# Holding the state-space scan's small matmuls in the program's order on TensorE

## The chip, the cores and the metric

The kernel runs on one core of a Trainium2 chip. The metric is the device time of one execution in microseconds; runs of the same kernel are summed up by their median.

## The reference, cut to what matters

One layer of a hybrid block: dilated attention and a state-space branch in parallel, on 256 positions of width 2048, float32 throughout. The change touches the scan of the state-space branch, which has 8 groups of 8 heads of 64 channels, with a state of 128:

```python
def step(state, inp):
    xc, dac, bc, cc = inp                       # chunks of 128 positions
    acum_t = jnp.moveaxis(jnp.cumsum(dac, axis=1), 1, -1)
    seg = acum_t[..., :, None] - acum_t[..., None, :]
    decay = jnp.exp(jnp.where(causal, seg, -jnp.inf))
    cb = jnp.einsum('blgn,bsgn->bgls', cc, bc)
    y_diag = jnp.einsum('bgls,bgjls,bsgjp->blgjp', cb, decay, xc)
    y_off = jnp.einsum('blgn,bgjpn,blgj->blgjp', cc, state, jnp.exp(acum))
    ...
    return new_state, y_diag + y_off
...
proj = rms_norm(x, norm_w) @ w_in               # q, k, v, z_a, z_s, xbc, dt, g_a, g_s
...                                             # conv and silu on xbc -> xs, B, C; dt = softplus
y = ssd_chunked_scan(xs * dt, dt * a, B, C) + d_skip * xs
y = rms_norm(y * silu(z_s), ssm_norm_w)
merged = sigmoid(g_a) * (o_a @ w_attn_branch) + sigmoid(g_s) * (y @ w_ssm_branch)
return rms_norm(x + merged @ w_out, final_norm_w)
```

The kernel doesn't carry a state from chunk to chunk: with two chunks it multiplies, for each head, the causal 256 x 256 matrix of C, B and decay with the inputs.

## The kernel before, in words

**Weights.** All weights stream from memory in units of 128 x 1024 floats, in one fixed order. ScalarE makes a rounded high part `h` of each unit (line 265) and VectorE the remainder `l` (line 266), into rings of four buffers each; TensorE multiplies with both parts. A projection of 128 output channels (`gemm_a`) reads two units: 16 pairs of an h matmul of 512 columns (line 318) and an l matmul of 256 columns (line 321) into one bank of PSUM.

**Groups.** For each of the 8 groups the program runs projections for B and C (groups 1 to 7), then by turns `xs` and `zs` for its four tiles of 128 channels. Between them stand a few gate projections (`gs`). Each projection begins with a tick of a counter. Work that must lie between projections is put on a list with the number of ticks to wait (`after`), and runs when the counter is there; with `inside=1` it is issued behind the first h matmul of a projection, ahead of that projection's first l matmul.

**The scan of a group.** Three ticks after a group's last `xs` projection has begun, `turn` transposes the inputs and makes `xdt`. `decays` (four calls, from the second tick on) makes the matrices `gt` on ScalarE and, per two calls, one VectorE multiplication (line 760). Eleven ticks after (some more where gate projections stand between), `scan` issues 16 matmuls, all on line 788, into two banks `yp`. Each takes 64 stationary columns, so that it writes 64 partitions: index `j` says which half, and neighbours in the source write different halves. Each is two records in the trace. Behind the scan, `gather` reads the sums on VectorE (line 800).

**What sets the order.** The source gives the program's order. The context is opened with `schedule_with_timeline_sim=True`: the framework simulates a timeline and issues on each engine, whenever that engine is free in the simulation, the first instruction in the program's order that is ready there. So an instruction whose inputs are ready may be issued ahead of its place in the source, into a pause of its engine in the simulated timeline. On the chip each engine then runs its queue in the order so fixed, with semaphores for the data.

Of the kernel before, what the change touches and what calls it, by code (L numbers as in the profile page):

```python
# [186 lines left out]
def hybrid_block(ctx: ExitStack, tc: tile.TileContext, wall, xt, x, pk_d, cst_d, fw_d, out):  # L187
    nc = tc.nc
    ve, ac, gp, pe = nc.vector, nc.scalar, nc.gpsimd, nc.tensor

    lead = ctx.enter_context(tc.tile_pool(name="lead", bufs=1))
    big = ctx.enter_context(tc.tile_pool(name="big", bufs=1))
# [20 lines left out]
    def bank(tag, bufs, name):  # L213
        return ps.tile([P, 512], F32, name=name, tag=tag, bufs=bufs)
# [77 lines left out]
    def after(ticks, f, inside=0):  # L292

        due.append((now[0] + ticks + inside / 2, f))
# [359 lines left out]
    with tc.tile_pool(name="ssm", bufs=2) as sp:  # L654
# [125 lines left out]
        def scan(g, state):  # L780
            xdt, gt = state["xdt"], state["gt"]
            yps = [bank("m2", 2, f"yp{g}_{v}") for v in range(2)]
            for k in (3, 2, 1, 0):
                v, i = divmod(k, 2)
                for a, b, c, o in ((0, S, 0, 0), (S, 384, 1, P)):
                    for j in range(2):
                        n, rows, col = 2 * i + j, 64 * j, i * S + o
                        pe.matmul(
                            yps[v][rows : rows + 64, col : col + b - a], xdt[:, v, c, n, :], gt[:, 4 * v + n, a:b],
                            start=(c == 0), stop=(c == 1),  # L790
                        )
            for v, yp in enumerate(yps):
                after(Y_AFTER[v], lambda a=(2 * g + v, yp, state["xs"][v], state["zs"][v]): gather(*a))

        def gather(u, yp, xs, zs):
            if True:
                y1 = sp.tile([P, 2, S], F32, name=f"y1_{u}", tag="y1", bufs=1)
                for i in range(2):
                    t = 2 * u + i
                    ve.scalar_tensor_tensor(  # L800
                        y1[:, i], xs[:, i], dsk[:, t : t + 1], yp[:, i * S : (i + 1) * S], ALU.mult, ALU.add
                    )
                ve.tensor_tensor(y1, y1, zs, ALU.mult)
                ac.activation(xs, y1, AF.Square)
                ve.tensor_tensor(ssq, ssq, xs, ALU.add)
                if u in (8, 12):
                    yT.append(half_kts(f"yT1{u}", "yo1a" if u == 8 else "yo1b"))
                for i in range(2):
                    t = 2 * u + i
                    split(y1[:, i], kt_of(yT, t)[:, :S], kt_of(yT, t)[:, S:], scale=nw[:, t : t + 1])  # L810
# [65 lines left out]
        for g in range(GROUPS):  # L876
# [9 lines left out]
            for t in range(max(4 * g, 1), 4 * g + 4):  # L886
                u, i = divmod(t, 2)
                acc = project(("xs", t))
                if i == 0:
                    state["xs"].append(new_pair(u, "xs"))  # L890
                if t % 4 == 3:
                    gate = 4 * len(GS_BEFORE.get(g + 1, ()))
                    after(TURN_LAG + gate * 3 // 4, lambda a=(g, state): turn(*a))

                    y_lag = Y_LAG + gate
                    for k in range(4):
                        after(GT_LAG + k if k < 3 else y_lag - 2, lambda a=(g, k, cb, state): decays(*a))
                    after(y_lag, lambda a=(g, state): scan(*a), 1)
                    for q in (2 * g, 2 * g + 1):
                        if q in SX_Y:  # L900
                            after(
                                y_lag + 2 + Y_AFTER[1] + q % 2 * 3,
                                lambda q=q, g=g: keep_left(
                                    ("y", q), two_kts(yT, q), Y_SPARE[q], at if g < 6 else ring(f"sxt_y{q}")
                                ),
                            )
                conv(collect(acc, f"x{t}"), t, state["xs"][-1][:, i], f"x{t}")
                acc = project(("zs", t))
                if i == 0:
                    state["zs"].append(new_pair(u, "zs"))  # L910
                zh = ev.tile([P, S], F32, name=f"zh{t}", tag="eh", bufs=2)
                evac(acc, zh, f"z{t}", scale=0.5)
                half_silu(zh, state["zs"][-1][:, i], f"z{t}")
# [260 lines left out]
```

## Time and profile before

| | |
|---|---|
| median of 3 runs | 1389.33 us (1388.9 to 1390.08) |
| the profiled execution's own time | 1389.12 us |
| its span, first to last instruction | 1387.3 us |
| granted TensorE clock | 0.998 |
| TensorE busy | 1376.8 us, 99% of the span |
| VectorE busy | 1148.3 us, 83% |
| ScalarE busy | 828.9 us, 60% |
| scan matmuls (line 788) | 256 records, first at 164.4 us, last at 584.5 us |

PE is TensorE, PEld its weight loads, DVE is VectorE, ACT is ScalarE, POOL is GpSimd, SP is SyncE. A row of the timeline has the start and the duration in us, then engine, line, operation, the tile written and those read, the shapes, and how many were merged into the row. Matmuls overlap in a pipeline and their ends are modelled, so a matmul's cost is read from start to start. A row of the waits view has who waited for whom, then the total in us, the number of times and the longest.

### The profile page before, as it was taken

The numbers are of one execution on the slowest core, as the hardware profiler recorded it, in microseconds if no ns is written. First come the engines' busy times: TensorE is split into PE (matmuls) and PEld (weight loads), VectorE is DVE, ScalarE is ACT, GpSimd is POOL, SyncE is SP. The second block draws the span as 40 slices with busy tenths as digits, with TensorE's granted clock in tenths as the row PEclk, the third lists the DMA queues.
The fourth block names the chain that finished last, engine by engine and source line by source line (L and its number), as shares of the span: only waits on it lengthen the run. The fifth ranks groups of instructions, "written<-read, shape, count | busy, mean of one in ns | idle before, by whom it ended". The sixth has DMA issues, their size and how long they took to land.

```text
span 1387.3 us, 20558 instructions
## 1 busy us (share of the span) xinstructions
PE 1376.8 (99%) x7272; PEld 1171.5 (84%) x7272; DVE 1148.3 (83%) x1709; ACT 828.9 (60%) x1289; POOL 130.3 (9%) x201
## 2 busy tenths in 40 slices
PE   9999999999999999999999999999999999999997
PEld 7888888888888888888888888888888888888886
DVE  6898998887798888868878997777777688889897
ACT  7656677675677675765554554544544456556464
POOL 2301110010000000010000001111111000000110
PEclk9999999999999999999999999999999999999999
DMA  9766877868676866567767668888888656776764
GB/s 346 231 189 213 285 241 236 272 200 300 217 251 212 261 197 204 186 228 267 237 224 258 224 195 287 275 274 277 296 287 279 182 171 219 270 250 207 251 241 150
DMA packets 100743, 332.67 MB, mean 240 GB/s; under 512 B 11232, under 2 KB 13472, under 8 KB 100512
## 3 DMA queue, kind: packets, MB, share of 16 engines
q1 hardware_dynamic: 99920, 330.18, 72.0%
q8 instruction: 57, 0.93, 0.3%
q10 hardware_dynamic: 720, 1.18, 0.2%
q14 instruction: 46, 0.38, 0.1%
HBM read 306.87 MB, written 24.44 MB: 239 GB/s over the span
## 4 chain that ended last, share of the span: by engine, by line
PE 98%; DMA 0%; DVE 0%; POOL 0%; SPq 0%; ACT 0%; issue 0%; POOLq 0%; DVEq 0%; ACTq 0%
PE ps_zs L318 8%; PE ps_xs L318 8%; PE ps_zs L321 4%; PE ps_q L318 4%; PE ps_k L318 4%; PE ps_za L318 4%; PE ps_xs L321 4%; PE ps_ssm L463 3%; PE ps_ssm L464 3%; PE ps_ssm L465 3%; PE ps_q L321 2%; PE ps_k L321 2%; PE ps_za L321 2%; PE ps_gs L402 2%; PE ps_gs L403 2%; PE ps_gs L401 2%
## 5 line engine op out<-in xcount | busy, mean ns | idle before, releaser
L265 ACT ACTIVATE h<-w 128x1024 fp32r<-128x1024 f32 (+1 forms) x408 | 425.7, 1049 | 357.2 <-issue 82.8
L266 DVE TENSOR_TENSOR l<-w,h 128x1024 fp32r<-128x1024 f32 (+1 forms) x408 | 491.9, 1211 | 160.9 <-ACT h L265 158.5
L318 PE MATMUL ps_zs<-XT,h 128*128 128x512 f32 x496 | 175.7, 395 | 0.0
L318 PE MATMUL ps_xs<-XT,h 128*128 128x512 f32 x496 | 175.2, 394 | 0.0
L321 PE MATMUL ps_zs<-XT,l 128*128 128x256 f32 x496 | 139.6, 282 | 0.0
L321 PE MATMUL ps_xs<-XT,l 128*128 128x256 f32 x496 | 139.6, 281 | 0.0
L318 PEld LDWEIGHTS ps_xs<-XT,h 128*128 128x128 f32 x496 | 93.0, 188 | 21.3
L318 PEld LDWEIGHTS ps_zs<-XT,h 128*128 128x128 f32 x496 | 93.1, 188 | 20.9
L321 PEld LDWEIGHTS ps_zs<-XT,l 128*128 128x128 f32 x496 | 93.6, 189 | 1.9 <-issue 1.1
L321 PEld LDWEIGHTS ps_xs<-XT,l 128*128 128x128 f32 x496 | 93.6, 189 | 0.8 <-issue 0.6
L318 PE MATMUL ps_q<-XT,h 128*128 128x512 f32 x256 | 92.3, 404 | 0.0
L318 PE MATMUL ps_k<-XT,h 128*128 128x512 f32 x256 | 89.8, 394 | 0.0
L318 PE MATMUL ps_za<-XT,h 128*128 128x512 f32 x256 | 89.5, 394 | 0.0
L321 PE MATMUL ps_q<-XT,l 128*128 128x256 f32 x256 | 71.0, 277 | 0.0
L321 PE MATMUL ps_k<-XT,l 128*128 128x256 f32 x256 | 71.0, 277 | 0.0
L321 PE MATMUL ps_za<-XT,l 128*128 128x256 f32 x256 | 70.9, 277 | 0.0
L318 PEld LDWEIGHTS ps_k<-XT,h 128*128 128x128 f32 x256 | 48.0, 188 | 11.1
L318 PEld LDWEIGHTS ps_za<-XT,h 128*128 128x128 f32 x256 | 48.0, 188 | 11.0
L318 PEld LDWEIGHTS ps_q<-XT,h 128*128 128x128 f32 x256 | 48.0, 188 | 10.9
L751 ACT ACTIVATE gt<-acb,acT 128x128 f32<-128x128 f32 x128 | 43.8, 391 | 19.5 <-DMA acb<-acum_d 16.4
L512 ACT ACTIVATE ha<-wa 128x1024 fp32r<-128x1024 f32 x38 | 40.0, 1054 | 20.8 <-DMA wa<-in_wall 7.4
L513 DVE TENSOR_TENSOR ltu<-wa,htu 128x1024 fp32r<-128x1024 f32 x38 | 46.4, 1222 | 5.8 <-ACT htu L512 5.4
(633 smaller groups left out, 3270.2 us busy)
## 6 DMA issues: line engine op xcount, KB each, us to landing
w<-in_wall SPq DMA_DIRECT2D x404, 512.0 KB, 4.5
wa<-in_wall SPq DMA_DIRECT2D x38, 512.0 KB, 4.4
th_a<-in_wall SPq DMA_DIRECT2D x18, 512.0 KB, 5.5
acb<-acum_d SPq DMA_DIRECT2D x32, 256.0 KB, 3.8
wb<-in_wall SPq DMA_DIRECT2D x30, 256.0 KB, 3.7
sums_at<-in_wall SPq DMA_DIRECT2D x12, 512.0 KB, 4.0
t_ssm<-sums_at SPq DMA_DIRECT2D x12, 512.0 KB, 4.3
wt<-t_ssm SPq DMA_DIRECT2D x12, 512.0 KB, 4.9
```

Source lines behind the costliest of these rows:

```text
L265: ac.activation(h[:, a:b], w[:, a:b], AF.Copy)
L266: ve.tensor_tensor(l[:, a:b], w[:, a:b], h[:, a:b].bitcast(F32), ALU.subtract)
L318: pe.matmul(acc, h[:, kk, :], m, start=(kt == 0), stop=False)
L321: pe.matmul(acc[:, S:], l[:, kk, :], m[:, :S], start=False, stop=(kt == KT - 1))
L401: pe.matmul(accs[i], xh, h[:, kk], start=(kt == 0), stop=False)
L402: pe.matmul(accs[i], xh, l[:, kk], start=False, stop=False)
L463: pe.matmul(acc, xh, h, start=start, stop=False)
L464: pe.matmul(acc, xh, l, start=False, stop=False)
L465: pe.matmul(acc, xl, h, start=False, stop=stop)
L512: ac.activation(h, src, AF.Copy)
L513: ve.tensor_tensor(l, src, h.bitcast(F32), ALU.subtract)
L751: ac.activation(g4[:, n, b], acb[:, j, b // 2 * P : b // 2 * P + P], AF.Relu, scale=-1.0, bias=sc[:, h : h + 1],)
```

## The change

Each matmul of the scan is passed through `tc.keep_in_program_order`. That adds an edge from the matmul to the instruction that the source wrote last before it on the same engine. The edge binds the order of issue alone: the matmul may not be issued ahead of that instruction. It adds no semaphore and doesn't wait for the other's result. The first matmul of a scan is thereby bound behind the first h matmul of the projection in which `scan` is called, and each of the other 15 behind the one before it. The instructions that follow the scan in the source are not bound.

```diff
     ve, ac, gp, pe = nc.vector, nc.scalar, nc.gpsimd, nc.tensor
+    in_order = tc.keep_in_program_order
...
                 for a, b, c, o in ((0, S, 0, 0), (S, 384, 1, P)):
                     for j in range(2):
                         n, rows, col = 2 * i + j, 64 * j, i * S + o
-                        pe.matmul(
-                            yps[v][rows : rows + 64, col : col + b - a], xdt[:, v, c, n, :], gt[:, 4 * v + n, a:b],
-                            start=(c == 0), stop=(c == 1),
+                        in_order(
+                            pe.matmul(
+                                yps[v][rows : rows + 64, col : col + b - a], xdt[:, v, c, n, :], gt[:, 4 * v + n, a:b],
+                                start=(c == 0), stop=(c == 1),
+                            )
                         )
```

## Prediction

> **What bounds the kernel now.** I read the page first, then the waits of TensorE, then the timeline of TensorE alone around each place where the scan's matmuls (source line L788, tile `yp`) stand.
>
> ```profile
> span 1387.3 us, 20558 instructions
> ## 1 busy us (share of the span) xinstructions
> PE 1376.8 (99%) x7272; PEld 1171.5 (84%) x7272; DVE 1148.3 (83%) x1709; ACT 828.9 (60%) x1289; POOL 130.3 (9%) x201
> ```
>
> ```profile
> PE warm L592 <- DVE ssq L589: 1.4, 1, 1.4
> PE ps_first L366 <- ACT h L265: 0.7, 1, 0.7
> ```
>
> The first fence says that TensorE's rows cover 99% of the span. The second is the whole answer of the waits view for TensorE: 1.4 + 0.7 = 2.1 us of waiting, once each, both at the very start (warm-up matmuls and the first weight unit). So from there on the end of the kernel is set by what TensorE has in its queue and how long each piece takes. A microsecond taken out of that queue comes off the span, as long as the engines that feed it stay ahead.
>
> The Trainium skill speaks against reading it this way: "Trainium Kernel Development and Optimization", section "Performance Expectations", calls matmul busy time a bad metric because matmuls are pipelined, and names the share of weight loads among the good ones. By that, 84% stands for TensorE, there would be room on the engine, and the change would move nothing (my second case below). The trace's waits say otherwise, 2.1 us in all, and I go by them.
>
> How the scan stands among the projections, undisturbed (group 0; TensorE's timeline, the columns are start, duration, engine, line, operation, tiles, count):
>
> ```profile
> 163.78 0.39 PE L318 MATMUL ps_xs<-XT,h 128*128 128x512 f32 x1
> 164.01 0.28 PE L321 MATMUL ps_xs<-XT,l 128*128 128x256 f32 x1
> 164.12 0.39 PE L318 MATMUL ps_zs<-XT,h 128*128 128x512 f32 x1
> 164.44 2.82 PE L788 MATMUL yp<-gt,xdt 128*64 128x256 f32 x32
> 167.19 0.39 PE L321 MATMUL ps_zs<-XT,l 128*128 128x256 f32 x1
> 167.42 0.39 PE L318 MATMUL ps_zs<-XT,h 128*128 128x512 f32 x1
> ```
>
> The durations overlap, so I count from start to start. The projection's pitch, from one h matmul to the next with the l matmul between, is 164.12 - 163.78 = 0.34 us. With the scan between them the same step is 167.42 - 164.12 = 3.30 us. So one whole scan block (16 matmuls of the source, two records each, 32) costs 3.30 - 0.34 = 2.96 us of TensorE's time. In three groups the 32 don't stand together.
>
> ```profile
> 201.68 0.40 PE L318 MATMUL ps_zs<-XT,h 128*128 128x512 f32 x1
> 202.00 0.65 PE L788 MATMUL yp<-gt,xdt 128*64 128x256 f32 x2
> 202.58 0.39 PE L321 MATMUL ps_zs<-XT,l 128*128 128x256 f32 x1
> 202.80 0.40 PE L318 MATMUL ps_zs<-XT,h 128*128 128x512 f32 x1
> ```
>
> ```profile
> 225.62 0.40 PE L318 MATMUL ps_zs<-XT,h 128*128 128x512 f32 x1
> 225.94 2.81 PE L788 MATMUL yp<-gt,xdt 128*64 128x256 f32 x30
> 228.69 0.39 PE L321 MATMUL ps_zs<-XT,l 128*128 128x256 f32 x1
> 228.91 0.39 PE L318 MATMUL ps_zs<-XT,h 128*128 128x512 f32 x1
> ```
>
> Group 1: one matmul (x2) runs alone, four projections ahead of the other fifteen (x30). The block of 30 takes as long as one of 32.
>
> ```profile
> 260.64 0.39 PE L318 MATMUL ps_zs<-XT,h 128*128 128x512 f32 x1
> 260.96 0.86 PE L788 MATMUL yp<-gt,xdt 128*64 128x256 f32 x6
> 261.75 0.39 PE L321 MATMUL ps_xs<-XT,l 128*128 128x256 f32 x1
> 261.97 0.40 PE L318 MATMUL ps_xs<-XT,h 128*128 128x512 f32 x1
> ```
>
> ```profile
> 287.04 0.39 PE L318 MATMUL ps_zs<-XT,h 128*128 128x512 f32 x1
> 287.36 2.38 PE L788 MATMUL yp<-gt,xdt 128*64 128x128 f32 x26
> 289.67 0.38 PE L321 MATMUL ps_zs<-XT,l 128*128 128x256 f32 x1
> 289.89 0.40 PE L318 MATMUL ps_zs<-XT,h 128*128 128x512 f32 x1
> ```
>
> Group 2: three matmuls (x6) ahead, thirteen (x26) at the block's place.
>
> ```profile
> 523.96 0.39 PE L318 MATMUL ps_zs<-XT,h 128*128 128x512 f32 x1
> 524.27 0.65 PE L788 MATMUL yp<-gt,xdt 128*64 128x256 f32 x2
> 524.85 0.39 PE L321 MATMUL ps_xs<-XT,l 128*128 128x256 f32 x1
> 525.07 0.40 PE L318 MATMUL ps_xs<-XT,h 128*128 128x512 f32 x1
> ```
>
> ```profile
> 350.00:400.00 50.00, 2.82 (x32) 2.00 (x32) 1.00 0.69 221
> 400.00:450.00 50.00, 2.82 (x32) 2.00 (x32) 1.00 0.73 236
> 450.00:500.00 50.00, 2.82 (x32) 2.00 (x32) 1.00 0.73 225
> 500.00:550.00 50.00, 0.65 (x2) 0.19 (x2) 1.00 0.71 219
> 550.00:600.00 50.00, 5.64 (x62) 4.21 (x62) 1.00 0.59 193
> ```
>
> Group 6: again one matmul ahead. The last fence is the windows view of the scan's line (busy time and count on TensorE, then on its weight loads): groups 3, 4 and 5 are whole, and the blocks of 30 (group 6) and of 32 (group 7) are busy 5.64 us together, 2 x 2.82, so this block of 30 too costs what a whole one costs.
>
> **The change, part by part.** It removes, adds and lengthens no instruction. Each scan matmul gets an edge behind the TensorE instruction that the source wrote just before it. Such an edge orders issue only; it adds no semaphore and no wait. The first matmul of a scan is tied behind the first h matmul of the projection in whose midst the source puts the scan, the other fifteen behind one another. No DMA, and no instruction of another engine, is tied.
>
> What must go is the early start in groups 1, 2 and 6: the five matmuls (x2, x6, x2) can't be issued before their block's place any more. What I expect instead is eight blocks of 32.
>
> The sum, start to start, each less the pitch of 0.34:
> - Group 1: early part 202.80 - 201.68 - 0.34 = 0.78; block 228.91 - 225.62 - 0.34 = 2.95; together 3.73 against 2.96 for a whole block. Saved 0.77.
> - Group 2: early part 261.97 - 260.64 - 0.34 = 0.99; block 289.89 - 287.04 - 0.34 = 2.51; together 3.50. Saved 0.54.
> - Group 6: early part 525.07 - 523.96 - 0.34 = 0.77; block 2.96 as shown. Saved 0.77.
>
> In all 0.77 + 0.54 + 0.77 = 2.08 us.
>
> Why a lone matmul is so dear can be seen in the rows. At the whole block's rate two records are 2.96 x 2/32 = 0.19 us; alone they took 0.78. The shape column says 128*64: a scan matmul fills half of the array's columns, and in the source its neighbour fills the other half. Alone, the other half stands empty, and its partner later runs alone too, which is why a block of 30 is no shorter than one of 32. Besides, entering and leaving the half-width shape costs: from the last h start to the first scan start are 202.00 - 201.68 = 0.32 us, where from h to l in the plain stream are 164.01 - 163.78 = 0.23. And the first l after it is followed by h at 202.80 - 202.58 = 0.22, where it is 164.12 - 164.01 = 0.11 in the plain stream.
>
> The Trainium skill, "TensorEngine Tiling (Array Packing)", section "Key Properties", says that changing the tiling mode drains the TensorE. The rows agree: 0.32 against 0.23 us on entering. The page gives no figure for the drain; counting only the array's own time, the sum would be the busy difference that I give next.
>
> Both sides of the 2.08. From below: the busy times of the early parts, 0.65 + 0.86 + 0.65, less what the block of 26 is shorter than one of 32, 2.82 - 2.38 = 0.44, are 1.72 us; this leaves out the pauses of entering and leaving. From above: if the three matmuls put back in group 2 filled idle column halves, as the one in group 1 would, the block of 26 would not grow by 0.45, and the saving would be 2.53. I take 2.08, since the whole block was measured and holds all of its matmuls.
>
> What it costs elsewhere. The moved matmuls run later than now, by 24 us in group 1 and 26 us in group 2; their inputs were there at the early place, so nothing new is waited for at the later one. Each group's sums are read by VectorE after its last scan matmul, and that one stands where it stood. The wait that could newly appear is indirect. The kernel's order on every engine comes from a simulated timeline, in which the early matmuls filled pauses; without them that timeline shifts by some tenths of a microsecond after 202 us, and near-ties on VectorE, ScalarE and SyncE's queue may fall the other way. Ahead of 202 us the order should be unchanged. I cost this at nothing. The cover is the lead with which the weights' low parts are made:
>
> ```profile
> 245.83 1.22 DVE L266 TENSOR_TENSOR l<-w,h 128x1024 fp32r<-128x1024 f32 x1
> ```
>
> ```profile
> 249.35 0.19 PEld L321 LDWEIGHTS ps_xs<-XT,l 128*128 128x128 f32 x1
> ```
>
> These belong to the same unit of weights (counting units and l tiles in order), and this is the smallest lead that I find between 200 and 600 us: ready at 245.83 + 1.22 = 247.05, first loaded at 249.35, 2.30 us ahead. If some reordering delays an l by less than that, TensorE doesn't feel it; beyond it, every microsecond shows.
>
> The profiled execution took 1389.12 us, its span 1387.3 with 1.8 us around it; the median of the runs shown is 1389.33. So 1389.12 - 2.08 = 1387.0 for such an execution, and 1389.33 - 2.08 = 1387.2 for the median.
>
> **The rivals.**
> - *Nothing saved.* Either TensorE is not the bound and the 2.08 us turn into idle time, or the early pauses of the planner are filled by other matmuls of equal cost. Against it: the two waits above, and that the scan's are the only half-width matmuls in this stretch; full-width ones moved forward cost the same wherever they stand. 1389.3.
> - *Slower: the re-planned order makes VectorE late.* Place: VectorE between 202 and 600 us. Its longest pieces there are the multiplications of the decay matrices, two per group:
>
> ```profile
> L760 DVE TENSOR_TENSOR gt<-gt,cb 128x1536 f32<-128x1536 f32 x12 | 21.0, 1752 | 0.4 <-ACT gt L759 0.4
> ```
>
> If the two of a group (2 x 1.75) and the subtraction of another unit (1.22) came ahead of an l with the smallest lead, it would be 4.72 - 2.30 = 2.42 us late, and TensorE would stand for so long. It decides from 2.30 us of work moved ahead; it outweighs the saving from one group on. In three of the six groups from 2 to 7 it would be 7.26 - 2.08 = 5.2 us slower than now: 1394.5. For it: VectorE is busy 83% of the span. Against it: two such multiplications would have to fall together at the worst unit, after a shift of tenths of a microsecond.
>
> **How the numbers follow.** What a measurement of this kernel can tell from no change is about 0.2%, 2.8 us. The forecast, 1387.2, has 0.79; nothing saved 0.08; slower 0.13. The forecast saves 0.15%, within 0.7 us of the bound; the runs shown lie 1.18 us apart (1388.9 to 1390.08) and the saving may be 2.53, so I put a quarter of the forecast, 0.20, beyond it. Faster 0.20; within 0.2%: 0.59 + 0.08 + 0.01 of the slower case = 0.68; slower 0.12. The range: low is 1389.33 - 2.53 - 1.18 = 1385.6; high takes in nothing saved and the slower case with one group late, 1387.2 + 2.42 + 1.18 = 1390.8.
>
> **What would show it.** Right: the scan's line in eight runs of x32, with no x2, x6, x26 or x30, each step from h to h about 3.30; TensorE's waits still 2.1 us; TensorE's instructions as many as before; no difference ahead of 201 us; and group 2's block, after two early parts that are gone (0.78 and 0.99), starting at 287.36 - 1.77 = 285.6. Wrong: pieces of the scan still apart; new rows in TensorE's waits naming l or h; or a wait that isn't there now between 202 and 600 us. If the block's place itself moves within a projection, or the order after 600 us differs and costs, the forecast fails on the step that I costed at nothing.

## The result and the profile after

The changed kernel takes 1387.86 us in the median (22 runs, 1386.87 to 1389.66), the kernel before 1389.59 us (22 runs, 1388.9 to 1390.43). The ratio is 0.9987 with a 95% interval of 0.9981 to 0.9993. That is 1.73 us less, 0.13%, with an interval of 1.0 to 2.6 us: a real gain, but inside the 0.2% that the prediction counted as no change. The forecast was 1387.2 us, and its range, 1385.6 to 1390.8, held the time. Of the 0.66 us between forecast and median, 0.26 are the kernel before: its median over 22 runs is 1389.59, where the forecast had 1389.33 from three. The profiled execution took 1387.36 us against 1389.12 us before.

First the page of the changed kernel, then the whole answer of its waits view for TensorE, then from the waits of the weight loads the two rows that the text uses, and last the row of before that answers to the first of them. All lines of the source stand one to three lower than before: 788 is 790, 318 is 319, 321 is 322.

```profile
span 1385.5 us, 20557 instructions
## 1 busy us (share of the span) xinstructions
PE 1375.6 (99%) x7272; PEld 1171.3 (85%) x7272; DVE 1148.6 (83%) x1709; ACT 829.9 (60%) x1289; POOL 130.0 (9%) x201
```

```profile
PE warm L593 <- DVE ssq L590: 1.4, 1, 1.4
```

```profile
PEld yp L790 <- issue: 2.1, 8, 0.4
...
PEld ps_attn L465 <- DVE l L267: 0.3, 1, 0.3
```

```profile
PEld yp L788 <- issue: 3.1, 11, 0.4
```

TensorE has as many instructions as before, 7272, and still waits for almost nothing. The loads of `yp` paused for issue 11 times before, for 3.1 us in all; now they do so 8 times, once per block. The row of `ps_attn` is new: it has one weight load of the attention branch waiting for a low part `l`.

The scan's own rows, by the windows view of its line over the stretches that hold groups 1 and 2 and groups 6 and 7. The columns are the window, its length, TensorE's busy time and count, that of the weight loads, the clock, the DMA share and the GB/s. The first fence is before, the second after.

```profile
200.00:300.00 100.00, 6.71 (x64) 4.72 (x64) 1.00 0.76 245
500.00:600.00 100.00, 6.28 (x64) 4.40 (x64) 1.00 0.65 206
```

```profile
200.00:300.00 100.00, 5.64 (x64) 4.01 (x64) 1.00 0.75 251
500.00:600.00 100.00, 5.64 (x64) 4.00 (x64) 1.00 0.62 203
```

The same 128 records are busy 12.99 us before and 11.28 us after, 1.71 us less. Each stretch now costs twice 2.82 us. TensorE's timeline of the changed kernel shows the rest: the place where group 1's early matmul stood, then the blocks of groups 1, 2 and 6.

```profile
201.33 0.40 PE L319 MATMUL ps_zs<-XT,h 128*128 128x512 f32 x1
201.57 0.28 PE L322 MATMUL ps_zs<-XT,l 128*128 128x256 f32 x1
201.69 0.40 PE L319 MATMUL ps_zs<-XT,h 128*128 128x512 f32 x1
...
224.30 0.39 PE L319 MATMUL ps_zs<-XT,h 128*128 128x512 f32 x1
224.62 2.82 PE L790 MATMUL yp<-gt,xdt 128*64 128x256 f32 x32
227.37 0.39 PE L322 MATMUL ps_zs<-XT,l 128*128 128x256 f32 x1
227.59 0.39 PE L319 MATMUL ps_zs<-XT,h 128*128 128x512 f32 x1
...
284.91 0.40 PE L319 MATMUL ps_zs<-XT,h 128*128 128x512 f32 x1
285.24 2.82 PE L790 MATMUL yp<-gt,xdt 128*64 128x256 f32 x32
287.99 0.39 PE L322 MATMUL ps_zs<-XT,l 128*128 128x256 f32 x1
288.21 0.39 PE L319 MATMUL ps_zs<-XT,h 128*128 128x512 f32 x1
...
548.72 2.82 PE L790 MATMUL yp<-gt,xdt 128*64 128x256 f32 x32
```

At group 1's early place the step from h to h was 1.12 us (201.68 to 202.80); it is now 201.69 - 201.33 = 0.36. Its block takes 227.59 - 224.30 = 3.29 us, as the block of 30 did. Group 2's block has grown from 2.85 to 288.21 - 284.91 = 3.30 us. All eight groups show one run of x32.

I laid the two traces on one another, instruction by instruction, and read where the difference between their start times changes (after less before; estimates from single executions):

| where | change, us |
|---|---|
| start, before the first weight unit | -0.35 |
| group 1, early part gone | -0.76 |
| group 2, two early parts gone, block longer | -0.56 |
| group 6, early part gone | -0.77 |
| pitch of the projections and the transposes, up to 600 us | +0.27 |
| attention branch, at 1257 us | +0.39 |
| sum | -1.78 |

The spans differ by 1.8 us. The start is no effect of the change: the waits of TensorE for the first `h` are 0.7 us before, none here, and 1.4 us in a second profiled execution of the same changed kernel (below). Without it the table leaves -1.43 us. The start differs between executions in this way, so the trace alone doesn't set the net gain to better than some tenths; the medians do.

### The profile page after: what moved, and what is told of

It is laid out like the page before. It is cut to its first block, busy times and chain, and to the rows that moved or that the text cites. A ratio compares the mean times of both kernels' runs of the same rounds, so it can differ in the third digit from the quotient of the medians.

```text
span 1385.5 us, 20557 instructions
## 1 busy us (share of the span) xinstructions
PE 1375.6 (99%) x7272; PEld 1171.3 (85%) x7272; DVE 1148.6 (83%) x1709; ACT 829.9 (60%) x1289; POOL 130.0 (9%) x201
## 4 chain that ended last, share of the span: by engine, by line
PE 98%; DMA 0%; DVE 0%; POOL 0%; SPq 0%; ACT 0%; issue 0%; POOLq 0%; DVEq 0%; ACTq 0%
PE ps_zs L319 8%; PE ps_xs L319 8%; PE ps_zs L322 4%; PE ps_k L319 4%; PE ps_za L319 4%; PE ps_q L319 4%; PE ps_xs L322 4%; PE ps_ssm L465 3%; PE ps_ssm L464 3%; PE ps_ssm L466 3%; PE ps_q L322 2%; PE ps_k L322 2%; PE ps_za L322 2%; PE ps_gs L404 2%; PE ps_gs L403 2%; PE ps_gs L402 2%
```

## The experiments

Diffs are against the changed kernel, and so are differences in us; the ratios and intervals are against the kernel before. The questions were two. Why is a scan matmul that runs early so dear: because half of the columns stands empty, because of entering and leaving the half-width shape, or both? And what gave back part of the saving?

### One matmul early, in seven groups

```diff
+                    after(y_lag - 1, lambda a=(g, state): scan(*a, early=True), 1)
                     after(y_lag, lambda a=(g, state): scan(*a), 1)
...
+            for k, a, b, c, o, j in steps[:1] if early else steps[1:]:
```

> The changed kernel, but in groups 0 to 6 the first of the 16 scan matmuls is issued one projection ahead of the other 15 (both places held in the program's order), as the old order had it in groups 1 and 6. Seven such splits. Theory A (a split costs entering and leaving the half-width shape once more, about 0.34 us, and a lone use of half the array's columns, about 0.43 us): 7 x 0.77 = 5.4 us over the changed kernel, about 1393.3. Rival B (only entering and leaving costs): 7 x 0.34 = 2.4 us, about 1390.3. Rival C (only the lone half costs): 7 x 0.43 = 3.0, about 1390.9. Rival D (the splits were not what cost time; the gain came from another order on the other engines): within 1 us of 1387.9.

Measured: 1393.71 us (1392.86 to 1394.81), ratio 1.0029 (1.0018 to 1.0039), 5.85 us above the changed kernel. TensorE's timeline in group 0 (the scan's line is L794 here):

```profile
158.96 0.39 PE L319 MATMUL ps_xs<-XT,h 128*128 128x512 f32 x1
159.28 0.65 PE L794 MATMUL yp<-gt,xdt 128*64 128x256 f32 x2
159.85 0.39 PE L322 MATMUL ps_xs<-XT,l 128*128 128x256 f32 x1
160.08 0.40 PE L319 MATMUL ps_xs<-XT,h 128*128 128x512 f32 x1
...
165.29 0.39 PE L319 MATMUL ps_zs<-XT,h 128*128 128x512 f32 x1
165.61 2.81 PE L794 MATMUL yp<-gt,xdt 128*64 128x256 f32 x30
168.36 0.39 PE L322 MATMUL ps_zs<-XT,l 128*128 128x256 f32 x1
168.58 0.39 PE L319 MATMUL ps_zs<-XT,h 128*128 128x512 f32 x1
```

The early step is 160.08 - 158.96 = 1.12 us and the block's 168.58 - 165.29 = 3.29 us: the same numbers as in groups 1 and 6 of the kernel before, now made on purpose in seven groups. Seven times 0.77 is 5.4 us. So the splits cost what the prediction read from the rows.

### Two matmuls early, one for each half

The same edit with `steps[:2]` and `steps[2:]`.

> As the run with one scan matmul ahead, but the first two of the 16 go ahead, which write different halves of the array's columns. Theory A: no half stands empty, so only entering and leaving is paid a second time, 7 x 0.34 = 2.4 us over the changed kernel, about 1390.3; each block left behind is shorter than 2.96 us by about 0.43. Rival B (only entering and leaving costs): the same 1390.3, so this run and the one with one ahead would be equal. Rival C (only the lone half costs): 1387.9. Rival D: within 1 us of 1387.9.

Measured: 1389.98 us (1389.5 to 1392.77), ratio 1.0003 (0.9995 to 1.0012), 2.1 us above the changed kernel. The same timeline:

```profile
158.49 0.39 PE L319 MATMUL ps_xs<-XT,h 128*128 128x512 f32 x1
158.81 0.65 PE L794 MATMUL yp<-gt,xdt 128*64 128x256 f32 x4
159.39 0.39 PE L322 MATMUL ps_xs<-XT,l 128*128 128x256 f32 x1
159.61 0.40 PE L319 MATMUL ps_xs<-XT,h 128*128 128x512 f32 x1
...
164.82 0.39 PE L319 MATMUL ps_zs<-XT,h 128*128 128x512 f32 x1
165.15 2.39 PE L794 MATMUL yp<-gt,xdt 128*64 128x128 f32 x28
167.46 0.38 PE L322 MATMUL ps_zs<-XT,l 128*128 128x256 f32 x1
167.69 0.40 PE L319 MATMUL ps_zs<-XT,h 128*128 128x512 f32 x1
```

Four records take the same 0.65 us as two did, so the halves run beside one another, and the block is shorter by the pair: 167.69 - 164.82 = 2.87 us instead of 3.29. What is left per group is the visit to the half-width shape: 1.12 + 2.87 - 0.34 - 3.29 = 0.36 us, seven times 2.5. Both causes are real: an empty half is worth 5.85 - 2.1 = 3.7 us in seven groups (3.0 by the rows), and a visit more 2.1 to 2.5 us. "TensorEngine Tiling (Array Packing)" of the Trainium skill, section "Key Properties", tells of a drain on a change of mode. These rows agree that a change costs, some 0.35 us for going in and out; that all of it is the drain isn't shown.

### All of one half, then all of the other

```diff
-            for k in (3, 2, 1, 0):
+            for j in range(2):
+                for k in (3, 2, 1, 0):
```

> The changed kernel with the 16 scan matmuls of a group held in another order: first all eight that write partitions 0 to 63, then all eight that write 64 to 127. No neighbour fills the other half of the columns. If the two halves run at once only because neighbours in the program write different halves, a block's array time doubles from about 2.6 to 5.2 us, 8 x 2.6 = 20.8 us, about 1408.7. If the hardware pairs them whatever their order, 1387.9.

Measured: 1404.12 us (1403.62 to 1405.36), ratio 1.0105 (1.0091 to 1.0118), 16.3 us more: the direction is as expected, the size is 4.5 us short. Timeline of group 0:

```profile
164.46 4.82 PE L790 MATMUL yp<-gt,xdt 128*64 128x256 f32 x32
```

The block takes 4.82 us instead of 2.82, and eight times 2.0 are the 16 us. In the single records, the last four of the first half and the first four of the second run together, from 166.46 to 167.06, which saves 0.65 us a block against one half after the other. The records don't name their half; which is which is read from the program's order and from the spacing, 0.22 us between two of 256 columns of one half and 0.11 between two of 128. Read so, the second half's first record starts 6 ns after the thirteenth of the first half, while three that were queued ahead of it were still to come. The next kernel tests that.

### Half by half within each pair of heads

```diff
             for k in (3, 2, 1, 0):
                 v, i = divmod(k, 2)
-                for a, b, c, o in ((0, S, 0, 0), (S, 384, 1, P)):
-                    for j in range(2):
+                for j in range(2):
+                    for a, b, c, o in ((0, S, 0, 0), (S, 384, 1, P)):
```

> The changed kernel with the order of a pair of heads turned inside: first both matmuls (four records) that write the lower half of the partitions, then both that write the upper half, and so on. If TensorE starts matmuls strictly in queue order, the upper half's first can start only when the lower half's last has started, and most of each pair runs alone: about 1.08 in place of 0.65 us for a pair, 4 x 0.43 = 1.7 us a block, 8 x 1.7 = 13.8 us, about 1401.7. If a matmul for the free half may start ahead of up to four queued records of the busy half (as one stretch of 0.65 us in the run with eight and eight suggests), a block still costs 2.96 us: 1387.9.

Measured: 1388.32 us (1387.28 to 1389.32), ratio 0.9991 (0.9983 to 1.0), 0.46 us more. Timeline of group 0:

```profile
164.23 2.87 PE L790 MATMUL yp<-gt,xdt 128*64 128x256 f32 x32
```

The block is 2.87 us, 0.05 longer, though always four records of one half stand ahead of the four of the other. Had each matmul waited for the start of all before it, the expectation was 1401.7 us. In the single records the first of the second half starts at 164.240 us, 13 ns after the first of the four ahead of it, with the other three still to come. So here a matmul for the free half starts past three queued records of the busy one; the four of the expectation count in the one that has just started. Here the measurement differs from the Trainium skill: "TensorE: Matmul & The Clock Gate", section "Part 3: Packing small matmuls — row/col tiling", has matmuls start strictly in order.

### The changed kernel once more

No edit.

> The changed kernel as it is, beside the three others of this set. 1387.9 (1.7 us under the kernel before), and eight scan blocks of 32.

Measured: 1387.87 us (1387.08 to 1388.28), ratio 0.9987 (0.9978 to 0.9995). The median is that of the first time to 0.01 us. The profiled execution has a span of 1386.1 us, 0.6 longer. The waits of TensorE, whole answer, say where:

```profile
PE warm L593 <- DVE ssq L590: 1.4, 1, 1.4
PE ps_first L367 <- ACT h L266: 1.4, 1, 1.4
```

The wait for the first `h`, absent in the other execution, is 1.4 us here. From the first weight unit on the two executions run 0.64 to 0.65 us apart up to 1255 us, and 0.54 to 0.60 behind that. So what is told below of the projections' pitch belongs to the program and not to one execution.

### The small matmuls behind the l matmul

The traces, laid on one another, show that a projection's pair of h and l takes one of two times. TensorE's timeline before, the h matmuls of one projection of group 1, the first and the last of nine:

```profile
214.32 0.40 PE L318 MATMUL ps_zs<-XT,h 128*128 128x512 f32 x1
...
217.13 0.40 PE L318 MATMUL ps_zs<-XT,h 128*128 128x512 f32 x1
```

After, a projection in the same stretch:

```profile
213.21 0.39 PE L319 MATMUL ps_zs<-XT,h 128*128 128x512 f32 x1
...
215.98 0.39 PE L319 MATMUL ps_zs<-XT,h 128*128 128x512 f32 x1
```

Eight pairs take 2.81 us in the one and 2.77 in the other; over all projections the pair has about 353.2 or 346.7 ns. The value holds from projection to projection. Up to 600 us of the changed kernel it changes at 18 places. At 14 of them small matmuls stand between. At the other four none does: there the planner has issued an h matmul of the next projection ahead of an l matmul of this one, and the longer pair follows. The first of the four:

```profile
187.23 0.39 PE L319 MATMUL ps_xs<-XT,h 128*128 128x512 f32 x1
187.46 0.39 PE L319 MATMUL ps_zs<-XT,h 128*128 128x512 f32 x1
187.68 0.28 PE L322 MATMUL ps_xs<-XT,l 128*128 128x256 f32 x1
```

At four more places of this kind the value stays. By units of weights (8 pairs each), 71 of 152 units up to 600 us have the longer pair before and 78 after. Seven more units cost 7 x 8 x 6.5 ns = 0.36 us; the 0.27 in the table is the net of this and of the regrouped transposes. The same count settles what the two runs with early matmuls left over. They have 86 and 72 such units, 8 more and 6 fewer than the changed kernel, which is +0.4 and -0.3 us. Without it they stand 5.4 and 2.4 us above the changed kernel, as their rows say (5.4 and 2.5). This run moves the place of the small matmuls (of the scan, and of the products of C and B) within the projection:

```diff
+                pe.matmul(acc[:, S:], l[:, kk, :], m[:, :S], start=False, stop=(kt == KT - 1))
                 if kt == 0:
                     run_due(now[0] + 0.5)
-                pe.matmul(acc[:, S:], l[:, kk, :], m[:, :S], start=False, stop=(kt == KT - 1))
```

> The changed kernel with the scan, and the small matmuls of C and B, put behind the first l matmul of a projection instead of between its first h and l matmul. The traces show that the pitch of a pair of h and l matmuls is either 346.7 or 353.2 ns for many projections in a row, and changes only where small matmuls stand between. If the place between h and l is what throws it into the slow pitch, most projections would now have 346.7: 96 of 248 units of 8 pairs are slow in the changed kernel, so up to 96 x 8 x 6.5 ns = 5.0 us less, 1382.9. If the place is the wrong way round, up to 152 x 8 x 6.5 ns = 7.9 us more, 1395.8. If the place doesn't matter, within 1.5 us of 1387.9 with some other share of slow units.

Measured: 1389.53 us (1389.09 to 1390.09), ratio 0.9998 (0.9989 to 1.0007), 1.7 us more. 114 of the 152 units have the longer pair, 36 more than after: 36 x 8 x 6.5 ns = 1.9 us. The pitch (the time of one pair) does hang on where the small matmuls stand, and this place is the worse one, though far from the 7.9 us that the expectation gave as the most. Why, this doesn't say. The expectation's 96 of 248 slow units in the whole changed kernel are too many: by the count used here they are 81, of which 78 stand up to 600 us.

### The scan one tick later

```diff
-DT_LAG, CB_LAG, TURN_LAG, GT_LAG, Y_LAG, S_LAG, M_LAG = 2, 5, 3, 2, 11, 2, 2
+DT_LAG, CB_LAG, TURN_LAG, GT_LAG, Y_LAG, S_LAG, M_LAG = 2, 5, 3, 3, 12, 2, 2
```

> The changed kernel with the scan one projection later (lag 12 in place of 11, and the decay matrices of the next group one tick later, since they reuse the buffer that the scan reads). In all traces so far a whole scan block leaves the projections in the slow pitch (353.2 ns a pair), and the next block of transposes in the fast one (346.7 ns). From the scan to the transposes are now about 14 us, some 40 pairs; one projection later they stand about 6 us apart, some 16 pairs. If that holds, 6 or 7 groups x 24 pairs x 6.5 ns = about 1 us less: 1386.9. If the pitch does not follow the two blocks, within 0.7 us of 1387.9. If the later scan makes VectorE and ScalarE late, waits of TensorE on h or l appear and it is slower.

Measured: 1393.73 us (1392.04 to 1395.08), ratio 1.003 (1.0019 to 1.0042); 5.9 us more than the changed kernel, where about 1 us less was expected; it is the slower of the cases named. From the waits of TensorE:

```profile
PE ps_ssm L464 <- ACT h L266: 2.8, 1, 2.8
...
PE ps_ssm L465 <- DVE l L267: 0.5, 1, 0.5
```

The last group's scan and sums came one projection later, and the state-space branch's projection behind them stood waiting for its weights, 3.3 us in these two rows. Laid on the changed kernel's trace it falls back by 5.5 us between 575 and 603 us, of which the rows name these 3.3, and by another 1.5 us in the attention branch. (The profiled execution is the slowest of this kernel's six, 1395.08 us.) The longer pair stands in 86 units, not in fewer. On the pitch this run says nothing clean. It does show that the cover which the prediction put against late weights has an end in this stretch: with one projection more of delay TensorE waits, mostly for an `h` from ScalarE.

### Transposes and products of C and B held in order too

```diff
-            pe.matmul(p[:, :S], bt[:, :P], ct_, start=True, stop=True)
-            pe.matmul(p[:, S : S + P], bt[:, P:], ct_[:, P:], start=True, stop=True)
+            in_order(pe.matmul(p[:, :S], bt[:, :P], ct_, start=True, stop=True))
+            in_order(pe.matmul(p[:, S : S + P], bt[:, P:], ct_[:, P:], start=True, stop=True))
...
-                        pe.transpose(tp[:, o : o + P], state["xs"][v][:, i, c * P : (c + 1) * P], ident)
+                        in_order(pe.transpose(tp[:, o : o + P], state["xs"][v][:, i, c * P : (c + 1) * P], ident))
```

> The changed kernel with the transposes of a group and the two matmuls of C and B held in the program's order too. In group 4 the eight transposes then stand in one block (7 + 1 in the changed kernel). Full-width matmuls cost the same wherever they stand, so by theory A within 0.5 us of 1387.9; the share of slow-pitch projections may move the time by some tenths.

Measured: 1387.36 us (1386.63 to 1388.82), ratio 0.9984 (0.9975 to 0.9993). Its median is the lowest of all kernels here, 0.5 us below the changed one, but the intervals of the two overlap almost wholly, so that it is better isn't shown. In its trace 72 units have the longer pair (6 fewer, 0.3 us). The attention branch's row for `l` doesn't appear among the waits, but only because it is smaller: the two steps there (the first is shown below) that are 0.84 and 0.66 us in the changed kernel, and 0.57 before, are 0.65 and 0.71 here.

## Why the prediction was right, step by step

- **TensorE sets the end.** Right. Work taken out of its queue came off the time. The prediction also weighed a rule of the Trainium skill ("Trainium Kernel Development and Optimization", section "Performance Expectations") that reads room from the share of weight loads. As the prediction took it, with that share at 84%, nothing would have moved; the interval of 1.0 to 2.6 us excludes that.
- **What goes.** Right: five early matmuls gone, eight runs of x32, as many instructions of TensorE. Group 2's block starts at 285.24 us where 285.6 was forecast; the 0.35 us are the start's.
- **What the splits cost.** Right: 0.76 + 0.56 + 0.77 = 2.09 us in the traces, 2.08 forecast. The lower bound of 1.72 is what the busy times give, 1.71 measured: the rest of the cost lies in the pauses of entering and leaving, which no row counts as busy. The upper bound, that group 2's block would not grow, is out: it grew by 0.45 us.
- **Why a lone matmul is dear.** Right in both causes, shown by the two runs with early matmuls: 5.9 us for one matmul early in seven groups, 2.1 us for two.
- **The new order elsewhere, costed at nothing.** This is the term that was mis-sized: 0.66 us in the traces. The prediction had named a new row for `l` in the waits as a sign against it, and one came. The order did change after 202 us; for instance the eight transposes of group 2 start at 238.77 us instead of 243.39. But the cover that I named was for VectorE being late, and none of that came in the stretch up to 600 us. What came instead was on TensorE itself: +0.27 us net from the pitch of the projections and a regrouping of transposes, a cost that I had not thought of, since I took the pitch as one number, 0.34, and held that a full-width matmul costs the same wherever it stands. And +0.39 us fell at 1257 us, where the order of TensorE was the same as before:

```profile
1254.97 0.82 PE L1067 MATMUL mtp<-cst,th_s 128*128 128x128 f32 x6
1255.81 0.50 PE L465 MATMUL ps_attn<-l,oaTa 128*128 128x512 f32 x1
```

```profile
1257.14 0.82 PE L1064 MATMUL mtp<-cst,th_s 128*128 128x128 f32 x6
1257.71 0.48 PE L464 MATMUL ps_attn<-l,oaTa 128*128 128x512 f32 x1
```

From the transposes to the l matmul it is 0.84 us after (first fence) and 0.57 before: the new wait for `l`, and 0.1 us more at the next such place. So a low part was late after all, though in another stretch than the one I had searched for the smallest lead. It can be followed back to a transfer that ScalarE waited for (again after, then before):

```profile
1242.82 1.06 ACT L513 ACTIVATE htt<-wt 128x1024 fp32r<-128x1024 f32 x1 [2.70 <-DMA wt<-t_attn]
1244.54 1.06 ACT L512 ACTIVATE htt<-wt 128x1024 fp32r<-128x1024 f32 x1 [2.26 <-DMA wt<-t_attn]
```

The transfer was issued 2.17 us earlier than before (1237.74 against 1239.91 us), as TensorE was 2.17 us ahead there. But ScalarE could start only 1.72 us earlier: 5.08 us passed from the issue to its start, and 4.63 before. From there VectorE works without a pause and in the same order in both kernels, up to the `l`, which is ready at 1255.75 and was ready at 1257.47. Before, that was 0.21 us ahead of its first load at 1257.68, a tenth of the lead of 2.30 us that I had found for the stretch up to 600 us; the 0.45 us used it up. So at this place it isn't another order on VectorE that made the `l` late. Why the transfer took longer is open. In the nine traces of kernels with the edges it took 4.9 to 5.4 us, so it is hardly one execution's chance, but of the kernel before there is one trace alone, and no run took the wait away by itself.
- **The net.** 2.08 was forecast; the medians give 1.73, the traces 1.43 without the start. The difference to the forecast, 0.35, is inside the interval of the measurement. That the term put at nothing came out so small was not shown by the prediction: its lead of 2.30 us was no cover for either of the two costs.

Of the rivals, *nothing saved* is out by the interval. *VectorE late* did not come in its form (2.42 us in a group); a wait of that price came only in the run with the scan one tick later, and there for an `h` from ScalarE (2.8 us).

Left open: what gives the pair of h and l its two values; what made the transfer in the attention branch longer; and whether holding the other small matmuls in order is worth anything.

## What to carry to other kernels

When an engine is busy nearly throughout, read a small operation's price from the step between its neighbours and not from its own duration: a lone half-width matmul here showed 0.65 us busy, cost 0.77 us, and saved nothing at the place that it had left. A planner that moves one matmul into a simulated pause may split a packed group, so look in the timeline whether groups that belong together stand as one row with the full count. And when an edge changes a planned order, search every stretch of the kernel for the smallest lead, not only the one where the edge is: here it was 2.30 us in the one and 0.21 us or less in another.

## What the runs showed of the hardware that was not expected

- A matmul for the free column half starts past three queued records of the busy half: the block took 2.87 us instead of 2.82 with the halves in turns of four records, and 4.82 us with one whole half behind the other, where strict order would give 2.82 + 2.0 + 0.65 = 5.5.
- The pair of h and l has two lasting values, 346.7 and 353.2 ns. Up to 600 us it was the longer after every block of 30 or 32 scan records and the shorter after every set of eight transposes, in the kernel before and in the changed one. That is no rule: in the run with the halves in turns of four records it was the shorter after five of seven blocks of 32, and in four places over the runs with edits a set of transposes left the longer. The cause is open.
